# Twelve of 22 column groups of each up projection by seven products of block sums, in a float32 encoder block on one core

## The chip, the core and the metric

The kernel runs on one core of one Trainium2 chip. It is judged by device time in microseconds (us). A core has five engines that run beside each other, each with an instruction queue of its own that it works through in order: TensorE (PE in the profile; PEld is its weight load, which runs beside the matmul before it), VectorE (DVE), ScalarE (ACT), GpSimd (POOL) and SyncE (SP, which here only issues transfers). They wait for each other through semaphores. Operands lie in SBUF, matmul results in PSUM, which has eight banks of 128 x 512 float32 here.

## The reference, cut to what matters

One layer of a hybrid encoder on 256 tokens of 2048 features, float32. It begins and ends with a gated feed-forward network (FFN); the mixing layer and the cross-attention between them are not touched.

```
def swiglu(h, w_up, w_down):
    gate, up = jnp.split(h @ w_up, 2, axis=-1)
    return (jax.nn.silu(gate) * up) @ w_down
...
x = x + 0.5 * swiglu(rms_norm(x, ffn1_norm[l]), ffn1_w_up[l], ffn1_w_down[l])
...
x = x + 0.5 * swiglu(rms_norm(x, ffn2_norm[l]), ffn2_w_up[l], ffn2_w_down[l])
```

w_up is 2048 x 11264 (gate and up halves of 5632 columns), w_down is 5632 x 2048. Weights are read once per run, some 470 MB in all.

## The kernel before, in words

**Precision.** Every float32 matrix is split in two parts, h (rounded for the matmul) and l (the rest): `split` (L142) copies with ScalarE (L143) and subtracts with VectorE (L144). A float32 product is then three matmuls, h by h, h by l and l by h, which add up in PSUM; `three` (L396 to L404) issues them, with the activations as the stationary operand of 128 x 128 and the weights as the moving one.

**Pieces and steps.** In an FFN the 22 groups of an up projection are 256 gate and 256 up columns each. A group is four pieces: a piece is 1 MB of weights, 128 partitions x 2048 (four k tiles of 512 columns). The down projection has 11 blocks of four pieces, one for each quarter of the output. `ffn` (L411) goes through a list of steps, a piece each, which `ffn_order` (L45) makes: four steps of a group, and from time to time two blocks of the down projection, whose eight steps follow each other. Without fast groups an FFN has 88 up steps and 44 down steps, each of 24 matmuls of 512 columns (four k tiles, two halves of the tokens, three matmuls).

**Preparation.** `prepare` (L368) runs two pieces ahead: SP loads raw (three buffers), then the piece is split into an h and an l tile of 128 x 2048 (pools h and l, three buffers each, `FFN_POOLS`, L284). A buffer of raw is loaded again when its split has read it; one of h or l is written again when TensorE has read it. The transfer of a piece is issued by SP, in order.

**The end of a group.** After a group's fourth step `activate` (L421) computes silu(gate) x up from PSUM (ScalarE L429, VectorE L430); `turn` (L434), meant for two steps later, transposes the hidden block on TensorE (four transposes, L438) and splits it (L442, L443). A pair of down blocks is added into x from PSUM by VectorE (L514).

**The other branch.** The kernel has a second way to do a group, step kind "fast", which is not taken while FAST is 0. It treats two k tiles of activations and the group's 2 x 256 columns as 2 x 2 blocks. `operand_pairs` (L342) makes the activations' tiles; its inner `fast` adds four block sums of each pair (on VectorE, 128 x 128 each) and splits them. In `prepare` the weights' block sums go into a tile td, and h and l get seven blocks of 256 columns per pair of k tiles, so a fast piece fills two h and two l tiles. `ffn` issues the seven products by the table SEVEN (three matmuls of 256 columns each) into four banks, and after the fourth step adds the banks up on VectorE into a tile ev before `activate`.

**Order.** Each engine's order is not that of the source: a scheduler sets it when the kernel is built, and waits and buffers follow from it. The tiles of a piece alternate strictly among the three buffers.

**The FFNs' ends.** FFN1 begins with the load of x and its operands (`head_x`, `head_rest`, L525 to L541), quarter by quarter, mixed with the first four pieces; each quarter's source is a tile of the pool td. FFN2's operands are made while the attention's output projection runs.

Of the kernel before, what the change touches and what calls it, by code (L numbers as in the profile page):

```python
# [8 lines left out]
F32 = mybir.dt.float32  # L9
F32R = mybir.dt.float32r  # L10
ACT = mybir.ActivationFunctionType
ALU = mybir.AluOpType

P = 128
T = 256
# [3 lines left out]
FT = DFF // P  # L19
NU = DFF // 256  # L20
NB = FT // 4
FAST = 0
EPS = 1e-6
HEADS = 4
HD = D // HEADS
# [19 lines left out]
def ffn_order(fast):  # L45

    left = {"fast": fast, "up": NU - fast}  # L50
    begun = {"fast": None, "up": None}
    out, ended, down = [], [], []
    names = count()
    blocks = seen = 0

    def step(kind):
        if begun[kind] is None:
            begun[kind] = [next(names), 0]
            left[kind] -= 1
        g, i = begun[kind]  # L60
        out.append((kind, g, i))
        begun[kind] = [g, i + 1]
        if i == 3:
            ended.append(g)
            begun[kind] = None

    total = 4 * (NU + NB)
    while len(out) < total:
        fasts = sum(e[0] == "fast" for e in out)
        more = left["fast"] or begun["fast"]  # L70
        if more and fasts * (total - 12) < 4 * fast * (len(out) - 3):
            step("fast")
            continue
        if not down and not begun["up"]:
            ready = seen // 2 - blocks
            if ready >= 2 or (ready and not left["up"] and not more):
                n = min(2, ready)
                down = [("down", blocks, n, c, b) for c in range(4) for b in range(blocks, blocks + n)]
                blocks += n
        seen = len(ended)  # L80
        if down:
            out.append(down.pop(0))
        elif left["up"] or begun["up"]:
            step("up")
        elif more:
            step("fast")
    number = {g: i for i, g in enumerate(ended)}
    return [(e[0], number[e[1]], e[2]) if e[0] != "down" else e for e in out]
# [3 lines left out]
def block_kernel(ctx: ExitStack, tc: tile.TileContext, xT, xin, memT, vec, gfin, lruw, wu1, wd1, win, wv,  # L92
                 wab, wout, wq, wk, wvm, wo, wu2, wd2, out_):
    nc = tc.nc
    pe, dve, act, sp = nc.tensor, nc.vector, nc.scalar, nc.sync
# [9 lines left out]
    scoped = {}  # L105

    @contextmanager
    def scope(**pools):
        with ExitStack() as inner:
            for name, bufs in pools.items():  # L110
                scoped[name] = inner.enter_context(tc.tile_pool(name=name, bufs=bufs, reuse_waits="tile"))
            yield
            scoped.clear()

    def slot(dt=F32, name="slot"):
        return slots.tile([P, 1024], dt, name=name, tag="slot")
# [25 lines left out]
    def split(h, l, raw):  # L142
        act.activation(h, raw, ACT.Copy)  # L143
        dve.tensor_tensor(out=l, in0=raw, in1=h.bitcast(F32), op=ALU.subtract)  # L144
# [65 lines left out]
    def summed(acc, out=None, by=None):  # L210

        lo = t1("lo")
        act.activation(lo, acc[:, T:], ACT.Copy)
        out = t1("sum") if out is None else out
        dve.tensor_tensor(out=out, in0=acc[:, :T], in1=lo, op=ALU.add)
        if by is not None:
            dve.tensor_tensor(out=out, in0=out, in1=by, op=ALU.mult)
        return out
# [62 lines left out]
            dve.scalar_tensor_tensor(out=x[m], in0=half, scalar=by, in1=x[m], op0=ALU.mult, op1=ALU.add)  # L281


    FFN_POOLS = dict(h=3, l=3, td=2, ev=1, hd=2, tmp=4)  # L284

    class TokenSquares:

# [54 lines left out]
    def operand_pairs(src, gain, q, xg):  # L342

        out = []
        for i in range(2):
            for z in range(2):
                k = 2 * i + z
                act.activation(xg[i][:, z * T:][:, :T], src[:, k * T:(k + 1) * T], ACT.Copy,
                               scale=col(gain, 4 * q + k))
            h = slot(F32R, "xh")  # L350
            l = slot(F32R, "xl") if FAST else h[:, 512:]
            split(h[:, :512], l[:, :512], xg[i][:, :512])
            out.append((h, l))

        def fast():
            for s, (h, l) in zip(xg, out):
                for o, a, b, op in ((4, 1, 3, ALU.add), (5, 4, 0, ALU.subtract), (6, 1, 0, ALU.subtract),
                                    (7, 2, 5, ALU.subtract)):
                    o, a, b = (s[:, j * P:(j + 1) * P] for j in (o, a, b))
                    dve.tensor_tensor(out=o, in0=a, in1=b, op=op)  # L360
                split(h[:, 512:], l[:, 512:], s[:, 512:])

        return out, fast if FAST else lambda: None

    def split_pool(name):
        return scoped[name].tile([P, 2048], F32R, name=name, tag=name)

    def prepare(e, wu, wd, cuts=1):  # L368

        raw = rawp.tile([P, 2048], F32, name="raw", tag="raw")  # L370
        src = wd[e[4], e[3]] if e[0] == "down" else wu[e[1], e[2]]
        if e[0] != "fast":
            h, l = split_pool("h"), split_pool("l")
            n = 2048 // cuts
            for a in range(0, 2048, n):
                sp.dma_start(raw[:, a:a + n], src[:, a:a + n])
                split(h[:, a:a + n], l[:, a:a + n], raw[:, a:a + n])
            return h, l
        sp.dma_start(raw, src)
        out = []  # L380
        for i in range(2):
            b = raw[:, i * 1024:(i + 1) * 1024]
            td = scoped["td"].tile([P, 1024], F32, name="td", tag="td")
            b12, b22, b21 = b[:, :T], b[:, 512:768], b[:, 768:]
            dve.tensor_tensor(out=td[:, :512].rearrange("p (i n) -> p i n", i=2),
                              in0=b12[:, None, :].broadcast_to([P, 2, T]),
                              in1=b[:, 256:768].rearrange("p (i n) -> p i n", i=2), op=ALU.subtract)
            dve.tensor_tensor(out=td[:, 512:768], in0=b22, in1=td[:, :T], op=ALU.subtract)
            dve.tensor_tensor(out=td[:, 768:], in0=b21, in1=td[:, 512:768], op=ALU.subtract)
            h, l = split_pool("h"), split_pool("l")  # L390
            split(h[:, :768], l[:, :768], b[:, 256:])
            split(h[:, 768:1792], l[:, 768:1792], td)
            out.append((h, l))
        return out

# [15 lines left out]
    def ffn(order, wu, wd, pairs, sq, then, before=()):  # L411
# [42 lines left out]
        for e in order:  # L454
            while todo and len(ahead) < 2:
                i = len(order) - len(todo)
                if i < len(before):
                    before[i]()
                ahead.append(prepare(todo.pop(0), wu, wd, 4 if before and i == 0 else 1))
# [63 lines left out]
    fast1 = []  # L523

    def head_x(q):  # L525
        src = scoped["td"].tile([P, 1024], F32, name="xf", tag="td")
        n = 256 if q == 0 else 1024
        for a in range(0, 1024, n):
            sp.dma_start(src[:, a:a + n], xT[:, q * 1024 + a:][:, :n])
        new, fast = operand_pairs(src, "ffn1_norm", q, [slot(name="xg") for _ in range(2)])  # L530
        pairs1.extend(new)
        fast1.append(fast)

    def head_rest():
# [5 lines left out]
        for f in fast1:  # L540
            f()  # L541

    head = [lambda q=q: head_x(q) for q in range(4)] + [head_rest]


# [32 lines left out]
    xs2, sq2 = Operands(), TokenSquares()  # L578
    order1 = ffn_order(FAST)

# [7 lines left out]

    with scope(**FFN_POOLS):
        ffn(order1, wu1, wd1, pairs1, sq1, to_mix, head)  # L590
# [15 lines left out]
    def heads(t):  # L606
        return t.rearrange("p (h t) -> p h t", h=4)
# [3 lines left out]
    v = [scoped["extra"].tile([P, 1024], F32, name=f"v{t}", tag="extra") for t in range(2)]  # L611
# [230 lines left out]
    for m in range(KT):  # L842
# [3 lines left out]
        b = summed(parts[1], by=heads(gates[1, m // 4])[:, m % 4])  # L846
# [118 lines left out]

    with scope(**FFN_POOLS):
        ffn(ffn_order(FAST), wu2, wd2, pairs2, sq4, to_out)
        r = sq5.rstd_tokens()
# [96 lines left out]
```

## Time and profile before

| | |
|---|---|
| median of three runs | 2570.26 us (2565.64 to 2571.64) |
| the profiled execution: its own time, its span | 2569.93 us, 2568.2 us |
| TensorE busy, matmuls | 2531.1 us (99%), 12554 |
| VectorE, ScalarE busy | 1492.7 us (58%), 1209.3 us (47%) |
| chain that ended last | 95% TensorE |
| bytes read, mean rate | 470.10 MB, 184 GB/s |
| the two FFNs | about 7 to 757 us and 1821 to 2568 us of the span |

A row of the groups names line, engine, operation, out<-in, shapes and count; then total busy us, the mean ns of one, and the engine's idle time just before them with what ended it. A row of the timeline gives start and length in us, the engine, line, operation and tiles, xN for N merged ones, and in brackets the idle time before and who ended it. A matmul's length contains its way through the array, so consecutive ones overlap in the list; what one costs in a stream is the distance between starts. TensorE's granted clock is 0.995 of full speed on the mean.

### The profile page before, as it was taken

Reading aid. Unit: us, or ns where it says so; the run is one execution under the profiler, and the core shown is the slowest. Engines: PE = TensorE matmul, PEld = TensorE weight load, DVE = VectorE, ACT = ScalarE, POOL = GpSimd, SP = SyncE. Lnnn points to the kernel's source line nnn. Section 1 sums busy time; section 2 is a strip of 40 time slices with the busy share of each in tenths; the row PEclk is TensorE's granted clock in tenths of the full one; section 3 lists DMA queues with packets and bytes.
Section 4 is the critical chain, followed back from the end, with each engine's and each line's share of the span. In section 5 each row is a group of like instructions: output and inputs, shape, how many; then the busy total and the mean of one; then the engine's idle time right before and its main releaser. Section 6 shows DMA issues by size and latency. Waiting matters only on the chain.

```text
span 2568.2 us, 30319 instructions
## 1 busy us (share of the span) xinstructions
PE 2531.1 (99%) x12554; PEld 2132.7 (83%) x12554; DVE 1492.7 (58%) x1648; ACT 1209.3 (47%) x1416; POOL 0.2 (0%) x4
## 2 busy tenths in 40 slices
PE   7999999999999999999999999999999999999998
PEld 6888888888878888888888888888788888888886
DVE  5454545454555767776787776566445454545455
ACT  6434333434354444596555564555533334333333
POOL 0000000000000000000000000000000000000000
PEclk9999999999999999999999999999999999999999
DMA  7555555555535444454555555444555555555553
GB/s 267 193 187 194 192 186 195 188 189 196 183 146 196 164 164 151 166 178 178 186 191 190 204 200 194 164 148 164 190 187 195 184 194 191 186 196 187 191 195 133
DMA packets 68682, 474.16 MB, mean 185 GB/s; under 512 B 7616, under 2 KB 8384, under 8 KB 12352
## 3 DMA queue, kind: packets, MB, share of 16 engines
q1 hardware_dynamic: 68544, 472.23, 51.8%
q8 instruction: 98, 1.61, 0.2%
q14 instruction: 40, 0.33, 0.0%
HBM read 470.10 MB, written 2.10 MB: 184 GB/s over the span
## 4 chain that ended last, share of the span: by engine, by line
PE 95%; ACT 3%; DVE 1%; issue 0%; DMA 0%; SPq 0%; DVEq 0%; ACTq 0%
PE acc L198 20%; PE acc L404 19%; PE acc L402 18%; PE acc L403 18%; PE acc L199 10%; PE acc L656 2%; PE acc L658 2%; PE acc L657 2%; PE acc L438 1%; PE acc L720 1%; ACT wh L143 1%; ACT h L143 0%; DVE l L144 0%; ACT L796 0%; PE acc L932 0%
## 5 line engine op out<-in xcount | busy, mean ns | idle before, releaser
L144 DVE TENSOR_TENSOR l<-raw,h 128x2048 fp32r<-128x2048 f32 (+1 forms) x267 | 605.5, 2268 | 622.7 <-ACT h L143 621.6
L198 PE MATMUL acc<-ops,wh 128*128 128x512 f32 x2432 | 856.7, 397 | 1.0 <-ACT wh L143 0.9
L143 ACT ACTIVATE h<-raw 128x2048 fp32r<-128x2048 f32 (+1 forms) x267 | 506.4, 1897 | 733.7 <-PE acc L403 726.0
L199 PE MATMUL acc<-ops,wl 128*128 128x256 f32 x2432 | 680.7, 280 | 2.3 <-DVE wl L144 2.3
L144 DVE TENSOR_TENSOR wl<-raw,wh 128x1024 fp32r<-128x1024 f32 x352 | 430.2, 1224 | 264.8 <-ACT wh L143 262.7
L143 ACT ACTIVATE wh<-raw 128x1024 fp32r<-128x1024 f32 x352 | 372.4, 1059 | 414.8 <-PE acc L198 239.7
L402 PE MATMUL acc<-h,xh 128*128 128x512 f32 x1408 | 554.8, 394 | 11.5 <-ACT h L143 11.5
L404 PE MATMUL acc<-l,xh 128*128 128x512 f32 x1408 | 551.8, 392 | 5.3 <-DVE l L144 5.3
L403 PE MATMUL acc<-h,xh 128*128 128x512 f32 x1408 | 551.0, 391 | 0.0
L198 PEld LDWEIGHTS acc<-ops,wh 128*128 128x128 f32 x2432 | 456.7, 188 | 106.7 <-ACT wh L143 1.6
L199 PEld LDWEIGHTS acc<-ops,wl 128*128 128x128 f32 x2432 | 459.5, 189 | 4.1 <-DVE wl L144 3.6
L402 PEld LDWEIGHTS acc<-h,xh 128*128 128x128 f32 x1408 | 266.3, 189 | 67.3 <-ACT h L143 12.8
L404 PEld LDWEIGHTS acc<-l,xh 128*128 128x128 f32 x1408 | 266.2, 189 | 62.6 <-DVE l L144 6.7
L403 PEld LDWEIGHTS acc<-h,xh 128*128 128x128 f32 x1408 | 266.5, 189 | 54.5
L402 PE MATMUL acc<-h,hidop 128*128 128x512 f32 x704 | 275.2, 392 | 0.7 <-ACT hidop L442 0.7
L404 PE MATMUL acc<-l,hidop 128*128 128x512 f32 x704 | 274.3, 390 | 0.0
L403 PE MATMUL acc<-h,hidop 128*128 128x512 f32 x704 | 274.0, 389 | 0.0
L403 PEld LDWEIGHTS acc<-h,hidop 128*128 128x128 f32 x704 | 132.2, 188 | 27.8 <-DVE hidop L443 0.6
L402 PEld LDWEIGHTS acc<-h,hidop 128*128 128x128 f32 x704 | 132.1, 188 | 27.7 <-ACT hidop L442 1.1
L404 PEld LDWEIGHTS acc<-l,hidop 128*128 128x128 f32 x704 | 132.1, 188 | 27.6
L429 ACT ACTIVATE sg<-acc,rtok 128x256 f32<-128x256 f32 x88 | 40.9, 465 | 133.5 <-PE acc L404 133.5
L514 DVE SCALAR_TENSOR_TENSOR x<-acc,x 128x512 f32<-128x512 f32 x96 | 65.7, 691 | 37.6 <-PE acc L404 37.6
(189 smaller groups left out, 1352.4 us busy)
## 6 DMA issues: line engine op xcount, KB each, us to landing
raw<-wu SPq DMA_DIRECT2D x175, 1024.0 KB, 4.8
raw<-wd SPq DMA_DIRECT2D x88, 1024.0 KB, 4.8
raw<-win SPq DMA_DIRECT2D x72, 1024.0 KB, 4.8
raw<-wab SPq DMA_DIRECT2D x16, 1024.0 KB, 4.8
raw<-wout SPq DMA_DIRECT2D x16, 1024.0 KB, 4.8
raw<-wq SPq DMA_DIRECT2D x16, 1024.0 KB, 4.7
raw<-wk SPq DMA_DIRECT2D x16, 1024.0 KB, 4.8
raw<-wvm SPq DMA_DIRECT2D x16, 1024.0 KB, 4.7
```

The costliest lines, as they stand in the source:

```text
L143: act.activation(h, raw, ACT.Copy)
L144: dve.tensor_tensor(out=l, in0=raw, in1=h.bitcast(F32), op=ALU.subtract)
L198: pe.matmul(acc, h, x, start=start, stop=False)
L199: pe.matmul(acc[:, :T], l, x[:, :T], start=False, stop=stop)
L402: first = pe.matmul(acc, ah, bh, start=start, stop=False)
L403: pe.matmul(acc, al, bh, start=False, stop=False)
L404: return first, pe.matmul(acc, ah, bl, start=False, stop=stop)
L429: act.activation(sg, gate[t], ACT.Silu, scale=rstd[:, t:t + 1])
L514: dve.scalar_tensor_tensor(out=o, in0=accs["down"][t], scalar=0.5, in1=o, op0=ALU.mult, op1=ALU.add)
L656: pe.matmul(accs[t], xs[k][:, a:a + P], h, start=(k == 0), stop=False)
L657: pe.matmul(accs[t], xs[k][:, a:a + P], l, start=False, stop=False)
L658: pe.matmul(accs[t], xs[k][:, b:b + P], h, start=False, stop=(k == KT - 1))
```

## The change

FAST goes from 0 to 12: of each FFN's 22 groups, 12 are done by the fast branch. `ffn_order` spreads their 48 steps among the 40 remaining up steps and 44 down steps, after the first four steps of a group done the old way, so two steps in five are fast for most of an FFN (fast, other, fast, other, other). A fast step is 42 matmuls of 256 columns in place of 24 of 512. The weights' block sums of a whole piece are now made at once: td is one tile of 128 x 2048 in place of two of 1024, laid out like raw, so three VectorE instructions write all sums of a piece. The sources of x at the head of FFN1 come from the same pool, which now has one buffer. With FAST not 0, the l parts of the activations get tiles of their own, at the same columns as their h parts, and the block sums of the activations are made: in the head of FFN1, and for FFN2 in each quarter of the attention's output projection.

```
-FAST = 0
+FAST = 12
...
-    FFN_POOLS = dict(h=3, l=3, td=2, ev=1, hd=2, tmp=4)
+    FFN_POOLS = dict(h=3, l=3, td=1, ev=1, hd=2, tmp=4)
...
         sp.dma_start(raw, src)
+        td = scoped["td"].tile([P, 2048], F32, name="td", tag="td")
+        bv, tv = (v.rearrange("p (i j n) -> p i j n", i=2, j=4) for v in (raw, td))
+        dve.tensor_tensor(out=tv[:, :, :2], in0=bv[:, :, :1].broadcast_to([P, 2, 2, T]), in1=bv[:, :, 1:3],
+                          op=ALU.subtract)
+        dve.tensor_tensor(out=tv[:, :, 2], in0=bv[:, :, 2], in1=tv[:, :, 0], op=ALU.subtract)
+        dve.tensor_tensor(out=tv[:, :, 3], in0=bv[:, :, 3], in1=tv[:, :, 2], op=ALU.subtract)
         out = []
         for i in range(2):
-            b = raw[:, i * 1024:(i + 1) * 1024]
-            td = scoped["td"].tile([P, 1024], F32, name="td", tag="td")
-            b12, b22, b21 = b[:, :T], b[:, 512:768], b[:, 768:]
...
             h, l = split_pool("h"), split_pool("l")
-            split(h[:, :768], l[:, :768], b[:, 256:])
-            split(h[:, 768:1792], l[:, 768:1792], td)
+            split(h[:, :768], l[:, :768], raw[:, i * 1024 + 256:(i + 1) * 1024])
+            split(h[:, 768:1792], l[:, 768:1792], td[:, i * 1024:(i + 1) * 1024])
             out.append((h, l))
...
-        src = scoped["td"].tile([P, 1024], F32, name="xf", tag="td")
+        src = scoped["td"].tile([P, 2048], F32, name="xf", tag="td")[:, :1024]
```

The built kernel has 96 fast steps: per step three block-sum instructions on VectorE (1024, 512 and 512 columns) and four splits (768 and 1024 columns, twice).

More of the change, by code (lines that the diff above doesn't have):

```diff
@@ L379, in prepare @@
         sp.dma_start(raw, src)
+        td = scoped["td"].tile([P, 2048], F32, name="td", tag="td")
[4 more added lines that the diff above has]
+        dve.tensor_tensor(out=tv[:, :, 3], in0=bv[:, :, 3], in1=tv[:, :, 2], op=ALU.subtract)
         out = []
         for i in range(2):
-            b = raw[:, i * 1024:(i + 1) * 1024]
-            td = scoped["td"].tile([P, 1024], F32, name="td", tag="td")
-            b12, b22, b21 = b[:, :T], b[:, 512:768], b[:, 768:]
[L385 to L389, printed above, removed]
             h, l = split_pool("h"), split_pool("l")
-            split(h[:, :768], l[:, :768], b[:, 256:])
-            split(h[:, 768:1792], l[:, 768:1792], td)
+            split(h[:, :768], l[:, :768], raw[:, i * 1024 + 256:(i + 1) * 1024])
+            split(h[:, 768:1792], l[:, 768:1792], td[:, i * 1024:(i + 1) * 1024])
             out.append((h, l))
```

## The prediction

> **What bounds the kernel now.** I read the page first (busy shares, then the chain that ended last), then busy time by stage, then the groups kept apart by shape, and last the instructions in order of time where a price was wanted.
>
> ```profile
> span 2568.2 us, 30319 instructions
> ...
> PE 2531.1 (99%) x12554; PEld 2132.7 (83%) x12554; DVE 1492.7 (58%) x1648; ACT 1209.3 (47%) x1416; POOL 0.2 (0%) x4
> ...
> PE 95%; ACT 3%; DVE 1%; issue 0%; DMA 0%; SPq 0%; DVEq 0%; ACTq 0%
> ```
>
> TensorE carries 95% of the chain, so a change pays if it shortens TensorE's queue and leaves it fed. The two feed-forward stages (FFNs), the only place touched, are the first and last of these stretches (busy us of PE, PEld, DVE, ACT, POOL, then clock, DMA share, GB/s):
>
> ```profile
> 20.00:740.00 720.00, 715.15 (x3175) 589.54 (x3174) 361.06 (x244) 289.72 (x228) 0.00 (x0) 0.99 0.55 194
> ...
> 1840.00:2568.00 728.00, 716.69 (x3202) 592.37 (x3200) 366.17 (x257) 282.88 (x218) 0.00 (x0) 1.00 0.53 186
> ```
>
> There VectorE is half idle and ScalarE 60% idle. That idle time is what the change spends.
>
> **Prices.** Busy time of pipelined matmuls overlaps, so I take distances between starts.
>
> ```profile
> 199.76 0.39 PE L404 MATMUL acc<-l,xh 128*128 128x512 f32 x1
> ...
> 202.48 0.40 PE L404 MATMUL acc<-l,xh 128*128 128x512 f32 x1
> ```
> ```profile
> 1299.91 0.39 PE L198 MATMUL acc<-ops,wh 128*128 128x512 f32 x1
> ...
> 1303.37 0.39 PE L198 MATMUL acc<-ops,wh 128*128 128x512 f32 x1
> ```
> ```profile
> 864.87 0.39 PE L198 MATMUL acc<-ops,wh 128*128 128x512 f32 x1
> ...
> 865.93 0.40 PE L198 MATMUL acc<-ops,wh 128*128 128x512 f32 x1
> ```
> ```profile
> 862.62 1.87 PEld L720 LDWEIGHTS acc<-silu,k 128*128 128x128 f32 x16
> 864.41 0.19 PEld L198 LDWEIGHTS acc<-ops,wh 128*128 128x128 f32 x1
> ```
>
> The first pair is 12 matmuls of 512 columns apart: 2.72/12 = 0.2267 us each. The second is ten pairs of one 512 and one 256: 0.346 a pair, so a 256 costs 0.346 - 0.2267 = 0.119. The third, three such pairs, gives 0.353 and 0.127. The fourth: 16 weight loads under short matmuls in 1.79 us, 0.112 each, the floor for matmuls that each bring new weights. No row has 256 after 256; bounds 0.112 and 0.127, and I take 0.120, next to the ten-pair row, which has the same operand type.
>
> ```profile
> L144 DVE TENSOR_TENSOR l<-raw,h 128x2048 fp32r<-128x2048 f32 x263 | 602.8, 2292 | 621.4 <-ACT h L143 620.2 <-DMA x<-xin 1.1
> ...
> L143 ACT ACTIVATE h<-raw 128x2048 fp32r<-128x2048 f32 x263 | 503.9, 1916 | 732.1 <-PE acc L403 726.0 <-PE acc L198 4.1 <-DMA raw<-wu 2.1
> ...
> L144 DVE TENSOR_TENSOR wl<-raw,wh 128x1024 fp32r<-128x1024 f32 x352 | 430.2, 1224 | 264.8 <-ACT wh L143 262.7
> L143 ACT ACTIVATE wh<-raw 128x1024 fp32r<-128x1024 f32 x352 | 372.4, 1059 | 414.8 <-PE acc L198 239.7 <-issue 103.0 <-PE acc L658 50.2
> ...
> L514 DVE SCALAR_TENSOR_TENSOR x<-acc,x 128x512 f32<-128x512 f32 x96 | 65.7, 691 | 37.6 <-PE acc L404 37.6
> ...
> L430 DVE SCALAR_TENSOR_TENSOR hid<-acc,rtok,sg 128x256 f32<-128x256 f32 x88 | 42.3, 481 | 58.6 <-ACT sg L429 58.6
> ...
> L443 DVE TENSOR_TENSOR hidop<-acc,hidop 128x512 fp32r<-128x512 f32 x44 | 30.1, 684 | 2.7 <-ACT hidop L442 2.7
> ...
> L215 DVE TENSOR_TENSOR gate<-acc,lo 128x256 f32<-128x256 f32 x32 | 13.4, 418 | 1.7 <-ACT lo L213 1.7
> ...
> L144 DVE TENSOR_TENSOR xh<-xg,xh 128x512 fp32r<-128x512 f32 x16 | 11.1, 691 | 6.4 <-ACT xh L143 6.2
> ...
> L143 ACT ACTIVATE xh<-xg 128x512 fp32r<-128x512 f32 x16 | 10.1, 628 | 0.4
> ...
> L738 DVE TENSOR_TENSOR tots<-tots 128x128 f32<-128x128 f32 x2 | 0.6, 286 | 0.0
> ```
>
> VectorE: 0.69 for 512 columns, 1.22 for 1024, halfway, 0.96, for 768, 0.29 for 128. ScalarE: 1.06 for 1024, about 0.85 for 768 (between 0.63 and 1.06).
>
> **TensorE, per step.** A step of an up or down projection is 24 matmuls of 512: 5.44 us. A fast piece is 2 x 7 products of 3 matmuls, 42 of 256: 5.04 us. Gain 0.40; 96 fast pieces (12 groups x 4 x 2 FFNs): **-38.7** (-71 at 0.112, -10 at 0.127).
>
> The Trainium skill, page "TensorE: Matmul & The Clock Gate", section "Back-to-back issue gap", gives N/2.4 + 2.5 ns a warm matmul, 109 and 216 ns here. By it a fast piece would save 0.59 us and the sum would be -57; the 0.2267 us measured for 512 stands 11 ns above that rule.
>
> **Preparation.** An ordinary piece: one split, ScalarE 1.92 then VectorE 2.29. A fast one: block sums 1.22 + 2 x 0.69, then four splits, VectorE 2 x (0.96 + 1.22): 6.96 together, and ScalarE 2 x (0.85 + 1.06) = 3.8.
>
> ```profile
> 1822.99 0.69 DVE L144 TENSOR_TENSOR xh<-xg,xh 128x512 fp32r<-128x512 f32 x1 [2.34 <-ACT xh L143]
> 1823.60 2.29 DVE L144 TENSOR_TENSOR l<-raw,h 128x2048 fp32r<-128x2048 f32 x1
> ```
> ```profile
> 302.53 1.92 ACT L143 ACTIVATE h<-raw 128x2048 fp32r<-128x2048 f32 x1 [3.52 <-PE acc L403]
> ```
> ```profile
> 304.48 2.29 DVE L144 TENSOR_TENSOR l<-raw,h 128x2048 fp32r<-128x2048 f32 x1 [3.15 <-ACT h L143]
> ```
> ```profile
> raw<-wu SPq DMA_DIRECT2D x175, 1024.0 KB, 4.8
> ```
>
> Unwaiting VectorE work overlaps by 0.08 us, so a fast piece takes it 6.6. In the order of steps a group is ten steps: four fast, six ordinary. VectorE per group: 4 x 6.6 + 6 x 2.2 = 39.6; emptying four banks 3 x 0.69 + 0.42 = 2.5; 1.8 hidden blocks at 2 x 0.48 + 0.68 = 3.0; four residual adds 2.8: 48 us. TensorE: 4 x 5.04 + 6 x 5.44, and transposes (0.44 per hidden block, as before) 53.6. VectorE goes from half to nine tenths busy and still isn't the bound on average, so what counts is order.
>
> Walk through one group. With three h and l buffers and two per fast piece, the ordinary step behind a fast one can be split only from the fast step's start: 1.92 + 0.03 + 2.29 = 4.24 us, wanted at 5.04 + 0.45 (its third matmul is the first to read l). That fits by 1.2 us. But at two of four fast steps the built order puts the block sums of the next fast piece in front of that split on VectorE, and they wait for a transfer that starts only when the running piece's own raw was read. In the tightest case, counting from the start of the group's last fast step, the read ends at -2.45 (the buffer of its second half is free one ordinary step earlier, at -5.44; ScalarE's 0.85 lie beside VectorE's work on the first half, 0.96 and 1.22, which ends at -3.4; then 0.96), the transfer lands at 2.35 (4.8 us), sums to 3.6, split to 5.85, wanted at 5.49: 0.36 late. Then the banks: copy c, 0.69, an ordinary split 2.29 between, 0.42, 0.69, and sums of the next piece (2 x 0.69) woven in, 0.69, a split 0.96, hid 2 x 0.48: hid is done at 13.4, and the transposes, which stand after eight matmuls of the second ordinary step, reach TensorE at about 12.7: 0.6 lost with both waits; a second hidden block behind a 2.29 split loses 0.3. So 1.3 us where up pieces stand behind the group; with down pieces raw is read at -3.3 and nothing or 0.3 is lost. Over all I take 0.7 a group: **+17** for 24 groups (bounds 0 and 2.2 a group, +53, the rival below). Queued behind the late sums are that l split, the bank emptying and all later splits.
>
> **FFN1 start.**
>
> ```profile
> 26.57 2.29 DVE L144 TENSOR_TENSOR l<-raw,h 128x2048 fp32r<-128x2048 f32 x1 [1.11 <-DMA x<-xin]
> ```
> ```profile
> 17.14 0.50 PE L402 MATMUL acc<-h,xh 128*128 128x512 f32 x1 [2.26 <-ACT h L143]
> ```
> ```profile
> 37.44 0.39 PE L404 MATMUL acc<-l,xh 128*128 128x512 f32 x1
> 39.51 0.50 PE L402 MATMUL acc<-h,xh 128*128 128x512 f32 x1 [1.68 <-ACT h L143]
> ...
> 48.35 0.48 PE L402 MATMUL acc<-h,xh 128*128 128x512 f32 x1
> ```
> ```profile
> 17.00:25.00 8.00, 6.73 (x17) 5.10 (x18) 6.72 (x6) 7.87 (x15) 0.00 (x0) 0.58 0.97 346
> ...
> 41.50:46.00 4.50, 4.17 (x11) 3.34 (x12) 4.50 (x4) 1.92 (x2) 0.00 (x0) 0.62 0.69 248
> ```
>
> The fifth step starts at 39.51 now and the sixth at 48.35, the latter after a pause and a half clock that also go. In the changed order the fifth is the first fast piece. Behind the fourth split (done at 28.9, some 0.5 later now) VectorE has eight sums at 0.29, six operand splits at 0.69, the piece's block sums 2.6, two splits 0.96, an ordinary one 2.29, then the wanted 1.22: 14.4, and about 2 of waits for ScalarE: 45.7. TensorE, ready at 38.7 (37.7 now), idles 6.5 us and resumes at half clock (as the rows show after 2.3 us): fast piece done at 52.7, sixth step at 58.6, against 48.35 + 5.44 = 53.8 now. **+5** (3 to 10; the xT loads, now one buffer, also follow each other).
>
> **FFN2 start.** The last quarter's three more sums and one more operand split stand ahead of the first l split, which TensorE already waits for:
>
> ```profile
> 1825.94 1.22 PE L404 MATMUL acc<-l,xh 128*128 128x512 f32 x2 [3.14 <-DVE l L144]
> ```
>
> 3 x 0.29 + 0.69 = 1.6, and 1 for the other quarters: **+2.5** (0 to 4). The other quarters' work lies under 5.5 us per output tile of TensorE, of which VectorE uses some 3.3. Transfers, bytes and the down projections stay as they are, 0.
>
> **Sum.** -38.7 + 17 + 5 + 2.5 = -14.2, against the profiled execution's own 2569.93 us; the median 2570.26 is 0.3 above. 2556.
>
> **Rivals.** The first row is the transfers of the first 60 us.
>
> ```profile
> raw<-wu SPq DMA_DIRECT2D x11, 1024.0 KB, 7.9
> ```
>
> (1) Slower: the sums at the head of VectorE's queue. Place: the two fast steps per group, 48 in all, where they precede an ordinary split. For it: VectorE nine tenths busy, only 1.2 us of cover, and the same transfer at 7.9 us where many are in flight. Against: it lands in 4.8 in all steady parts, and DMA is half idle there. I have 8 us of the 17 for these places (0.17 each); 0.45 each brings no change, and 0.93 each (+44.6) gives 2592. (2) No change: a 256 at 0.1225 and 0.85 lost per group: -28.6 + 20 + 7.5, 2569. For it: the 0.127 row. (3) The 256 runs at the load floor 0.112: -71, with 1.05 lost per group (less cover) and 7.5: 2532. (4) Loads don't overlap: 42 x (0.112 + 0.120) = 9.7 us a fast step, +413, 2983. By that a 512 would take 0.34, and the rows show 0.227. The Trainium skill, same page, section "The mechanism", says that a weight load overlaps a running matmul only when its row group differs, which is this rival; the trace disagrees at full-height matmuls. That the change doesn't do what it says: the built order has 96 x 42 matmuls of 256 columns, so no.
>
> **Chances.** Forecast 0.43, (1) 0.33, (2) 0.15, (3) 0.08, (4) 0.01. Faster by over 0.2% (about what a measurement here can tell from no change, 5 us) is forecast and (3), 0.51; within 0.15; slower 0.34. Range 2530 to 2592: forecast, (2), most of (1) and of (3). The forecast's own range is 2545 to 2566 (0.1185 to 0.121 us, 0.5 to 0.95 per group).
>
> **What would show it.** Starts of L400 to L402 matmuls 0.12 apart and a fast step of 5.04; TensorE waits for l and hid under 1 us, few per group; a pause of some 6 us near 39 us. Wrong if waits for DVE l after fast steps sum to over 30 us, if VectorE waits for raw landings in the middle of the FFNs, if half-clock stretches appear there, or if the 256 lies outside 0.117 to 0.123.

## The result, and the profile after

The changed kernel takes 2540.39 us (median of four runs, 2538.34 to 2542.70), the kernel before 2570.70 us (median of four). The ratio is 0.9886, 95% interval 0.9869 to 0.9903: 30 us faster. The forecast was 2556, in the range 2530 to 2592. What TensorE gains came out as forecast; a loss that was forecast beside it did not come, so the sum was 16 us too high. The time also lies outside the forecast's own narrower range, 2545 to 2566. The profiled execution is the slowest of the four, 2542.7 us with a span of 2540.6; the profiled one of before had 2569.93 and 2568.2.

The page of the changed kernel's profiled execution (span, busy times, engines on the chain that ended last), and its busy time by stage with the columns as before:

```profile
span 2540.6 us, 35172 instructions
...
PE 2501.9 (98%) x14282; PEld 2188.1 (86%) x14282; DVE 1960.3 (77%) x2400; ACT 1390.9 (55%) x1744; POOL 0.2 (0%) x4
...
PE 95%; ACT 2%; DVE 1%; DMA 1%; issue 0%; DVEq 0%; ACTq 0%
```
```profile
60.00:740.00 680.00, 679.04 (x3959) 599.81 (x3958) 566.97 (x571) 361.19 (x369) 0.00 (x0) 1.00 0.54 194
```

TensorE still carries 95% of the chain. In the steady part of FFN1 it is busy 679 of 680 us at full clock, while VectorE has gone up to 83% (567 us). So the fast branch shortened TensorE's queue and did not starve it.

One fast step in the timeline (start, length, engine, line), from its first matmul to the first of the ordinary step behind it:

```profile
73.29 0.28 PE L400 MATMUL acc<-h,xh 128*128 128x256 f32 x1
73.41 0.28 PE L401 MATMUL acc<-h,xl 128*128 128x256 f32 x1
73.53 0.28 PE L402 MATMUL acc<-l,xh 128*128 128x256 f32 x1
...
78.21 0.28 PE L402 MATMUL acc<-l,xh 128*128 128x256 f32 x1
78.33 0.40 PE L400 MATMUL acc<-h,xh 128*128 128x512 f32 x1
```

42 matmuls take 78.33 - 73.29 = 5.04 us, 0.120 each. The median of the 96 fast steps is 5.033, of the ordinary steps before 5.440, so a fast step saves 0.407 us.

How long TensorE's sequence of steps took, from the starts of its matmuls (us):

| | before | after | difference |
|---|---|---|---|
| FFN1, start of its first step to the end of the sixth | 7.1 to 53.9 | 7.1 to 57.35 | +3.4 |
| FFN1, from there to the end | 702.5 | 682.2 | -20.3 |
| between the FFNs | 1065.2 | 1071.3 | +6.1 |
| FFN2, first step | 11.3 | 12.2 | +0.95 |
| FFN2, the rest | 724.05 | 705.2 | -18.9 |
| behind the last step | 11.25 | 12.35 | +1.1 |

The sum is, to rounding, the difference of the spans, 2540.6 - 2568.2 = -27.6. One of the rows is a surprise: in the stage between the FFNs TensorE has the same instructions in both kernels and took 6.1 us more. More on that at the end.

The steady parts hold 95 fast steps, 95 x 0.407 = 38.7, and became 39.2 us shorter. **On balance the groups lost nothing.** What TensorE's weight loads waited for in the steady part of FFN1 (who, for what: us in total, times, longest), and then VectorE:

```profile
PEld acc L325 <- DVE x L512: 1.5, 4, 0.5
PEld acc L325 <- issue: 1.2, 2, 0.6
PEld acc L402 <- DVE l L144: 1.1, 2, 0.8
PEld acc L436 <- DVE hid L428: 0.5, 2, 0.2
```
```profile
DVE l L144 <- ACT h L143: 51.9, 48, 3.2
DVE td L382 <- DMA raw<-wu: 26.3, 14, 3.8
```

VectorE does stand at the head of its queue waiting for transfers, as forecast (14 times in this stretch, 1.9 us each). But that wait reached TensorE almost nowhere: 1.1 us for l.

### The profile page after: what moved, and what is told of

Same layout as the page of the kernel before. It is cut to its first block, busy times and chain, and to the rows that moved or that the text cites. A ratio compares the mean times of both kernels' runs of the same rounds, so it can differ in the third digit from the quotient of the medians.

```text
span 2540.6 us, 35172 instructions
## 1 busy us (share of the span) xinstructions
PE 2501.9 (98%) x14282; PEld 2188.1 (86%) x14282; DVE 1960.3 (77%) x2400; ACT 1390.9 (55%) x1744; POOL 0.2 (0%) x4
## 4 chain that ended last, share of the span: by engine, by line
PE 95%; ACT 2%; DVE 1%; DMA 1%; issue 0%; DVEq 0%; ACTq 0%
PE acc L198 22%; PE acc L402 18%; PE acc L401 18%; PE acc L400 18%; PE acc L199 11%; PE acc L654 2%; PE acc L655 2%; PE acc L656 2%; PE acc L436 1%; PE acc L718 1%; DMA xf<-xT 1%; DVE l L144 0%; ACT wh L143 0%; PE acc L930 0%; PE acc L885 0%
## 5 line engine op out<-in xcount | busy, mean ns | idle before, releaser
L143 ACT ACTIVATE h<-raw 128x768 fp32r<-128x768 f32 (+2 forms) x363 | 484.4, 1335 | 458.5 <-PE acc L401 306.0
L400 PE MATMUL acc<-h,xh 128*128 128x256 f32 (+1 forms) x1984 | 635.8, 321 | 12.8 <-ACT h L143 12.8
L402 PE MATMUL acc<-l,xh 128*128 128x256 f32 (+1 forms) x1984 | 635.8, 321 | 7.4 <-DVE l L144 7.3
L144 DVE TENSOR_TENSOR l<-raw,h 128x768 fp32r<-128x768 f32 (+2 forms) x363 | 564.7, 1562 | 97.6 <-ACT h L143 97.1
L401 PE MATMUL acc<-h,xl 128*128 128x256 f32 (+1 forms) x1984 | 634.2, 320 | 0.0
L400 PEld LDWEIGHTS acc<-h,xh 128*128 128x128 f32 x1984 | 381.0, 192 | 40.9 <-ACT h L143 13.6
L402 PEld LDWEIGHTS acc<-l,xh 128*128 128x128 f32 x1984 | 380.9, 192 | 36.3 <-DVE l L144 10.1
L401 PEld LDWEIGHTS acc<-h,xl 128*128 128x128 f32 x1984 | 380.8, 192 | 27.5
L143 ACT ACTIVATE h<-td 128x1024 fp32r<-128x1024 f32 x192 | 198.9, 1050 | 158.4 <-DVE td L385 158.4
L144 DVE TENSOR_TENSOR l<-td,h 128x1024 fp32r<-128x1024 f32 x192 | 232.2, 1219 | 19.5 <-ACT h L143 18.6
L400 PEld LDWEIGHTS acc<-h,hidop 128*128 128x128 f32 x704 | 132.4, 188 | 25.7
```

What stands on the lines that cost most here:

```text
L400: first = pe.matmul(acc, ah, bh, start=start, stop=False)
L401: pe.matmul(acc, al, bh, start=False, stop=False)
L402: return first, pe.matmul(acc, ah, bl, start=False, stop=stop)
```

## The experiments

The question was why the groups lost nothing where 0.7 us each was forecast. Theory A: the waits are there and the cover is a little larger than worked out, so it is thin, and order decides. Theory B: VectorE has idle time, and order matters little. The runs then went on to the start of FFN1 and to more fast groups. All times by stage below are from the starts of TensorE's matmuls in each run's own trace; the changed kernel has 732.5 us for FFN1 and 717.4 for FFN2.

### One block sum made twice

```diff
         dve.tensor_tensor(out=tv[:, :, :2], in0=bv[:, :, :1].broadcast_to([P, 2, 2, T]), in1=bv[:, :, 1:3],
                           op=ALU.subtract)
+        dve.tensor_tensor(out=tv[:, :, :2], in0=bv[:, :, :1].broadcast_to([P, 2, 2, T]), in1=bv[:, :, 1:3],
+                          op=ALU.subtract)
```

> The first and largest of a fast piece's three block sums (1.22 us on VectorE) is made twice; nothing else changes. Theory A (thin cover): in the changed kernel the groups lose nothing because the l split behind a fast step is done 0.4 to 0.9 us before TensorE reads it at two of four fast steps, and hid 0.5 us before the transposes. 1.14 us more at the head of VectorE's queue overruns both, so about 0.24 + 0.6 at the splits and some 0.5 at the transposes, 1 to 1.3 us a group: 24 to 32 us over the changed kernel's 2540, 2560 to 2575, and the trace shows TensorE waiting for VectorE's l behind fast steps. Theory B (VectorE is a fifth idle in the feed-forward stages, so its order does not matter): 96 x 1.14 = 109 us of work go into the 270 us in which it is idle, under 3 us longer, 2540 to 2543.

2558.41 us, ratio to the kernel before 0.9954 (0.9939 to 0.9969): 18 us more than the changed kernel. FFN1 743.0, FFN2 727.1, 20 us more in the two. The timeline of this run, VectorE and TensorE at a second fast step of a group (in brackets the idle time before and who ended it; lines stand two lower in this kernel):

```profile
219.79 0.69 DVE L387 TENSOR_TENSOR td<-raw,td 128x512 f32<-128x512 f32 x1
221.61 2.36 DVE L144 TENSOR_TENSOR l<-td,h 128x1024 fp32r<-128x1024 f32 x2 [1.13 <-ACT h L143]
```
```profile
221.85 0.28 PE L403 MATMUL acc<-h,xl 128*128 128x256 f32 x1
222.89 0.39 PE L404 MATMUL acc<-l,xh 128*128 128x256 f32 x1 [0.76 <-DVE l L144]
```

(The doubled instruction writes the same values again.) TensorE waits for the split of the fast piece's own block sums (those of its first half), 0.9 us a time, at the second fast step of 11 of the 24 groups; one group in each stage loses 2.6, there at an ordinary piece, and the start of FFN1 ends 2.0 us later. So theory A holds in kind: 109 us of work put into VectorE's idle time cost 20 us, not 3. Its place was not the one I named. The scheduler built another order, which kept nearly all splits of the ordinary pieces in time, and the split of td, which mostly had 2.4 us to spare at that step in the changed kernel, was the one overrun.

### The block sums as they were

```diff
-    FFN_POOLS = dict(h=3, l=3, td=1, ev=1, hd=2, tmp=4)
+    FFN_POOLS = dict(h=3, l=3, td=2, ev=1, hd=2, tmp=4)
...
+            td = scoped["td"].tile([P, 1024], F32, name="td", tag="td")
+            b12, b22, b21 = b[:, :T], b[:, 512:768], b[:, 768:]
+            dve.tensor_tensor(out=td[:, :512].rearrange("p (i n) -> p i n", i=2),
+                              in0=b12[:, None, :].broadcast_to([P, 2, T]),
+                              in1=b[:, 256:768].rearrange("p (i n) -> p i n", i=2), op=ALU.subtract)
+            dve.tensor_tensor(out=td[:, 512:768], in0=b22, in1=td[:, :T], op=ALU.subtract)
+            dve.tensor_tensor(out=td[:, 768:], in0=b21, in1=td[:, 512:768], op=ALU.subtract)
```

> Twelve fast groups as in the changed kernel, but the block sums as before the change: per half of a piece, six instructions on two buffers of half the size, in place of three on one. VectorE has 2 x 0.69 + 4 x 0.42 = 3.06 us in place of 2.60 a piece, 44 us in all. Theory A (thin cover, 0.4 to 0.9 us at the tightest splits): 0.46 us more takes up nearly all of it, 0 to 0.4 us lost a group, 2540 to 2550; first-half sums stand alone at the head of the queue, which gives some back. Theory B (idle time covers it): 2540, within 2 us. The middle stage and the start of the second feed-forward stage stay as they are in the changed kernel by both.

So this run is the kernel before with FAST = 12 and nothing else changed. 2539.14 us, ratio 0.9882 (0.9867 to 0.9897), not to be told from the changed kernel. By stage it is 733.1 and 718.6, 1.7 us longer, as both theories allow; the middle stage was 4.4 us shorter here, by which the whole came out no slower. What the change gains is the twelve fast groups; the three large sums in place of six small ones bring 1.7 us by these two traces, which the whole times do not show.

### A later start, and then later transposes

```diff
-def ffn_order(fast):
+def ffn_order(fast, skip=3):
...
-        if more and fasts * (total - 12) < 4 * fast * (len(out) - 3):
+        if more and fasts * (total - 12) < 4 * fast * (len(out) - skip):
...
-    order1 = ffn_order(FAST)
+    order1 = ffn_order(FAST, 6)
```

> The order of steps of the first feed-forward stage alone: its first fast piece becomes the eighth step (near 59 us) in place of the fifth (38 us). All 96 fast steps stay. Theory A (the start costs 3.4 us net, because the first fast piece waits for VectorE's activation sums and block sums and then runs at half clock): the sixth step ends near 53.9 us as in the kernel before, and the whole is 3 to 4 us shorter, 2536 to 2537. Rival: the pause is the activation sums themselves, and the ordinary fifth and sixth steps find VectorE as late: no change within 1 us.

2547.52 us, ratio 0.9921 (0.9901 to 0.9941): slower than the changed kernel. Both theories missed. The start did gain, and more than hoped: the sixth step is done at 49.78 us, in place of 57.35, and of 53.91 before any change. But FFN1 as a whole took 742.2 us, 9.7 more. The waits of TensorE's weight loads in the steady part of FFN1, and a place in the timeline:

```profile
PEld acc L436 <- DVE hid L428: 13.0, 7, 5.0
PEld acc L436 <- issue: 5.5, 4, 1.8
```
```profile
322.33 0.39 PE L402 MATMUL acc<-l,hidop 128*128 128x512 f32 x1
323.98 0.33 PE L436 MATMUL acc<-vt,hid 128*128 128x128 f32 x1 [1.26 <-DVE hid L428]
```

Nine times (the expectation below has ten) TensorE stands before the transposes (L436) of a hidden block: from the matmul before to the transpose it is 1.3 to 1.8 us and once 4.9, where 0.23 is usual, 15.7 us in all. In the new order the scheduler had put these nine 24 matmuls behind the group's last fast step; in the changed kernel most stand 32 behind. Eight matmuls are 1.8 us, and that is about the wait. The next run moves only that.

```diff
-            late.append((2, lambda: turn(g, hid)))
+            late.append((3, lambda: turn(g, hid)))
```

> The later start of the run before (first fast piece as the eighth step of the first feed-forward stage), and in both stages the transposes of a hidden block are put into TensorE's queue one step later (after three steps in place of two). In the run with the later start alone TensorE stood before the transposes ten times in the first stage, 1.3 to 1.8 us each and once 4.9, because they stood 24 matmuls behind the last fast step in place of 32 and VectorE's hid came after them. Theory A (the loss is the place of the transposes): these 18 us go, the start's gain of 7.6 us (sixth step done at 49.8 in place of 57.35) stays, first stage 724 to 728 us in place of 742 and of 732.5 in the changed kernel, second stage 717 as it is; whole 2531 to 2537. Theory B (VectorE is simply late behind a fast group when a residual add falls there): the wait moves to the l splits behind, first stage over 735, whole over 2541.

2526.44 us, ratio 0.9833 (0.9816 to 0.9849): 14 us faster than the changed kernel, 44 faster than the one before. FFN1 723.8, FFN2 716.7. By the two traces 8.7 us of the gain over the changed kernel lie in FFN1, and 6.5 in the stage between the FFNs, which this edit does not touch. All that TensorE's weight loads still wait for in the same stretch of FFN1, hid no longer among it:

```profile
PEld acc L325 <- DVE x L512: 1.9, 5, 0.5
PEld acc L199 <- DVE wl L144: 1.4, 2, 1.1
PEld acc L325 <- issue: 1.2, 2, 0.6
PEld acc L198 <- ACT wh L143: 0.9, 1, 0.9
```

In FFN2, whose order of steps is that of the changed kernel, the edit changed hardly anything (717.4 in the changed kernel, 716.8 in the run with the later start). That it was not VectorE's order that got better can be read from the same traces. In the changed kernel, with the later start and here, hid is done 12.3 us after the start of its group's last fast step (median of the 24 groups); TensorE comes to the transposes at 12.3 us in the changed kernel (median), at 10.5 in all nine late cases of the run before, and at 15.95 here (median). Theory A: the loss was the place of the transposes, not VectorE's work.

### Fourteen fast groups

```diff
-FAST = 12
+FAST = 14
```

> 14 fast groups of 22 in place of 12, 16 fast steps more; the order becomes fast and ordinary steps in turn. TensorE gains 16 x 0.407 = 6.5 us. Theory A (thin cover): for a group of eight steps with two hidden blocks VectorE has 26.4 + 8.8 + 2.5 + 3 + 2.8 = 43.5 us against TensorE's 42.8, so it is the bound there, 0.7 to 1.5 us lost in each of 28 groups: 2553 to 2575, and TensorE waits for l. Theory B (average idle covers it, VectorE 639 us of 705 a stage): 2533 to 2535.

2572.67 us, ratio 1.0008 (0.9999 to 1.0017): the whole gain is gone. FFN1 748.7, FFN2 734.0, against 732.5 and 717.4, with 6.5 us less of matmuls. Theory A by its number, and again the wait is not the one named: TensorE (weight loads, then matmuls) stands for hid, hardly for l. (The two lists tell of the same waits, so 9.6 and 11.5 do not make the 21 us of which the next expectation speaks. From start to start the waits before late transposes are 12.8 us in FFN1 and 12.1 in FFN2.)

```profile
PEld acc L436 <- DVE hid L428: 9.6, 11, 1.8
PEld acc L436 <- issue: 6.3, 4, 1.8
PEld acc L400 <- ACT h L143: 4.5, 2, 2.2
...
PEld acc L402 <- DVE l L144: 1.0, 2, 0.6
```
```profile
PE acc L436 <- DVE hid L428: 11.5, 11, 1.4
```

So the same edit, transposes one step later, with 14 groups:

> 14 fast groups in each stage as in the run of that number, and the transposes one step later in TensorE's queue. With 14 alone the first stage took 748.7 us and the second 734.0, and TensorE waited 21 us for hid in the first. Theory A (place of the transposes): these waits go, 728 and 714 us, whole 2531 to 2537. Theory B (VectorE is the bound where fast and ordinary steps stand in turn, 43.5 us of work to TensorE's 42.8): the waits go over to l, half or more of the loss stays, whole 2545 to 2560.

2528.22 us, ratio 0.9844 (0.9827 to 0.9861); FFN1 726.8, FFN2 714.4. Theory A: one edit took some 42 us out of the two stages. 25 of them are the waits seen at the transposes; two waits for h of 2.0 us in each stage went too, and how these and the rest hang on the transposes was not followed. VectorE's busy time in the steady part of FFN1 (third of the busy columns), at 14 groups, first with the early and then with the late transposes:

```profile
60.00:740.00 680.00, 664.37 (x4027) 592.10 (x4026) 596.30 (x607) 364.52 (x369) 0.00 (x0) 1.00 0.55 192
```
```profile
60.00:740.00 680.00, 678.57 (x4120) 607.21 (x4118) 606.50 (x633) 378.55 (x405) 0.00 (x0) 1.00 0.56 194
```

VectorE is busier (89%) in the run that loses next to nothing than in the one that loses 20 us a stage (88%): it has the same work in a longer stage. The share said nothing about the loss; the order did.

### A sum on GpSimd

```diff
-        dve.tensor_tensor(out=tv[:, :, 3], in0=bv[:, :, 3], in1=tv[:, :, 2], op=ALU.subtract)
+        nc.gpsimd.tensor_tensor(out=tv[:, :, 3], in0=bv[:, :, 3], in1=tv[:, :, 2], op=ALU.subtract)
```

> As the kernel before it, and the third block sum of a fast piece (0.69 us on VectorE) is made by GpSimd, which is idle; no row shows what it takes there. Theory A (VectorE not the bound once the transposes stand later): no change to the kernel before it, within 3 us. Theory B (VectorE is the bound): 2.8 us of 43.5 go in each group, VectorE falls below TensorE's 42.8, and at up to about 2 us a sum on GpSimd most of the waits for l go, 2533 to 2540; at over 4 us a sum the last split of each half comes late and it is slower than the kernel before it.

2573.29 us, ratio 1.0015 (1.0003 to 1.0026): 45 us worse than the same kernel with the sum on VectorE. Neither theory. FFN1 748.7, FFN2 736.5. The groups by shape in the steady part of FFN1, VectorE's splits without and with the sum on GpSimd, and GpSimd's sum (busy us, mean ns):

```profile
L144 DVE TENSOR_TENSOR l<-raw,h 128x768 fp32r<-128x768 f32 x108 | 102.6, 953 | 0.7 <-ACT h L143 0.7
```
```profile
L144 DVE TENSOR_TENSOR l<-raw,h 128x768 fp32r<-128x768 f32 x108 | 121.2, 1125 | 0.0
```
```profile
L385 POOL TENSOR_TENSOR td<-raw,td 128x512 f32<-128x512 f32 x53 | 115.2, 2173 | 509.1 <-DVE td L384 431.5 <-ACT h L143 59.1 <-ACT sg L427 18.5
```

And this run's busy times in the same stretch (the fifth is GpSimd's):

```profile
60.00:740.00 680.00, 664.53 (x4029) 593.01 (x4028) 596.43 (x555) 363.45 (x369) 115.17 (x53) 1.00 0.56 192
```

36.5 us of sums (53 x 0.69) left VectorE in this stretch, and its busy time fell by 10.1 only, from 606.5 to 596.4, although the slower run has less of its stage in the stretch. Over the whole run, where the other work is the same, 77.1 us of sums left, and the lengths of all of VectorE's instructions together fell by 10.2: others of them got longer. Of 63 splits of 768 columns that met a sum on GpSimd, 29 took 2.05 us; one alone takes 0.95. And the sum itself takes 2.2 us there on the mean (0.69 on VectorE; a span on GpSimd is rough): 1.3 in 48 of the 112, over 3 in 41. It ends up on the way to the last split. The Trainium skill, page "SBUF — State Buffer", section "SBUF: two separate sides", says that a VectorE instruction with two SBUF inputs and a GpSimd one that reads SBUF shut each other out for the whole instruction; the doubled splits agree. How much of the 45 us is that and how much the order that the scheduler built for it was not separated.

### Both edits with 14, and 16 groups

```diff
-FAST = 12
+FAST = 14
...
-def ffn_order(fast):
+def ffn_order(fast, skip=3, rest=12):
...
-        if more and fasts * (total - 12) < 4 * fast * (len(out) - 3):
+        if more and fasts * (total - rest) < 4 * fast * (len(out) - skip):
...
-            late.append((2, lambda: turn(g, hid)))
+            late.append((3, lambda: turn(g, hid)))
...
-    order1 = ffn_order(FAST)
+    order1 = ffn_order(FAST, 6, 14)
```

> 14 fast groups in each stage, the first fast piece of the first stage as the eighth step, and the transposes one step later. Theory A (the terms add): the first stage as with the later start at 12 groups, 723.8, less 8 x 0.407 and plus about 1 us lost (as the second stage showed at 14: 714.4 against 716.7, 2.3 gained of 3.3), 721.5; second stage 714.4; 4.7 us less than 2526.4: 2520 to 2523, up to 5 more if the middle stage falls into its slower rhythm. Theory B (VectorE with hardly any idle time left makes the gains not add): 2526 or more in the same rhythm.

2527.61 us, ratio 0.9829 (0.9816 to 0.9842), not to be told from 12 groups with the same edits. Against that kernel FFN2 gained 3.2 us (713.5), more than forecast; FFN1 gained nothing (723.75) where 2.3 was, and the stage between them was 3.1 us longer. The gains add in one stage and not in the other. In FFN1 the trace shows a start that took 0.6 us more and three waits of 0.5 to 0.6 us, for l and hid, that the other kernel does not have; why they arise stays open.

With 16 and the transposes later, at the old start:

```diff
-FAST = 12
+FAST = 16
...
-            late.append((2, lambda: turn(g, hid)))
+            late.append((3, lambda: turn(g, hid)))
```

> 16 fast groups in each stage with the transposes one step later, the first fast piece as the fifth step as in the changed kernel. Now nine fast pieces of a stage follow a fast one directly. TensorE gains 32 x 0.407 = 13 us over 12 groups. Theory A (VectorE counts by queue, place by place): two fast pieces in a row ask 13.2 us of VectorE in 10.07 us of TensorE, about 2 us lost at each such pair, 36 us in all, slower than with 14: 2540 to 2560. Theory B (only the sum over a stage counts, 679 us of VectorE in 703): 2520 to 2527.

2552.29 us, ratio 0.9926 (0.9912 to 0.9939), theory A; FFN1 737.5, FFN2 724.8. In FFN1 two fast pieces follow each other at eight places (the expectation has nine). The largest waits, for h and then l, stand behind four of them, 2.3 us each:

```profile
214.60 0.50 PE L400 MATMUL acc<-h,hidop 128*128 128x512 f32 x1 [1.14 <-ACT h L143]
...
216.93 0.73 PE L402 MATMUL acc<-l,hidop 128*128 128x512 f32 x2 [0.88 <-DVE l L144]
```

The lowest median of all is that with 12 groups, a later start in FFN1 and the later transposes, 2526.44 us; 14 groups with one or both of these edits (2528.22 and 2527.61) cannot be told from it.

## Why the prediction was right where it was, and wrong where it was

**What bounds: right.** TensorE was the bound and stayed so. VectorE is busy 83% where the sum for a group gave nine tenths.

**Fast steps: right.** 0.120 us for a 256 was taken and 0.1198 measured; the term of -38.7 (-38.5 by its own prices) is 96 x 0.407 = -39.1. Rival (2) with 0.1225, rival (3), the load floor of 0.112, and rival (4), loads that don't overlap, are out.

**Groups: the step that failed.** +17 (0.7 a group) was taken, -0.5 for all 24 measured. (The -0.5 is what is left over of the steady parts. It holds 2.7 us of slower matmuls behind fast steps, told at the end, and some 3 us less of waits at the FFNs' ends.) This is a mis-sized term, and the walk can be checked against the trace at the very group it was made for, the first, whose last fast step starts at 83.79 us. VectorE:

```profile
79.47 0.95 DVE L144 TENSOR_TENSOR l<-raw,h 128x768 fp32r<-128x768 f32 x1
...
85.44 1.23 DVE L382 TENSOR_TENSOR td<-raw 128x1024 f32<-128x1024 f32 x1 [1.14 <-DMA raw<-wu]
...
86.98 2.28 DVE L144 TENSOR_TENSOR l<-raw,h 128x2048 fp32r<-128x2048 f32 x1
...
96.04 0.48 DVE L428 SCALAR_TENSOR_TENSOR hid<-ev,rtok,sg 128x256 f32<-128x256 f32 x1 [0.26 <-ACT sg L427]
```

And TensorE:

```profile
88.93 0.49 PE L436 MATMUL acc<-vt,hid 128*128 128x128 f32 x3
89.18 0.48 PE L400 MATMUL acc<-h,xh 128*128 128x512 f32 x1
89.50 0.39 PE L401 MATMUL acc<-h,xl 128*128 128x512 f32 x1
89.73 0.40 PE L402 MATMUL acc<-l,xh 128*128 128x512 f32 x1
```

| from the start of the group's last fast step | walk | trace |
|---|---|---|
| raw read to the end | -2.45 | -3.37 (80.42) |
| sums begin (transfer landed) | 2.35 | 1.65 |
| split of the ordinary piece done | 5.85 | 5.48 (89.27) |
| l wanted by TensorE | 5.49 | 5.94 (89.73) |
| hid done | 13.4 | 12.7 (96.52) |

The order and the wait for the transfer were right at this place. The read of raw ended 0.9 us earlier than walked, because VectorE was done earlier with the splits of that piece's first half; of this 0.37 us was left at the ordinary split, as the transfer took 5.0 us in place of 4.8 and half of another hidden block stood before the split. And TensorE came 0.45 later, mostly because the transposes of that hidden block (L436, 0.36 us) stand at the end of this fast step, which the walk had left out. So 0.36 late became 0.46 early, and hid, 0.7 late in the walk (13.4 against 12.7), was in time. The same holds elsewhere: at 22 of the 24 groups the split behind the last fast step is done 0.3 to 0.6 us before it is read. The lower bound of the term, 0, was the right value; the forecast put a loss of tenths into a place where an error of 0.8 us in the walk decides.

Rival (1), the sums at the head of VectorE's queue, got 0.33. Its wait stands at 29 places, not 48: behind the last fast step of 22 groups and the second of 7, since at the others the built order has the split first, or no fast piece follows. Its price was next to nothing: TensorE's weight loads wait 1.6 us for l in the steady parts of both FFNs. The runs with the doubled sum, with 14 and with 16 groups show that a loss of that size was near, a little more work or another order costing 18 to 44 us, but with waits at other places than the rival's: for the split of td, for hid, and behind two fast pieces in a row.

**FFN1 start: right in kind.** The sixth step was forecast to end at 58.6 and ended at 57.35, +3.4 against before where +5 was taken. The pause, and the clock (the column behind the five engines' busy times):

```profile
38.40:43.00 4.60, 1.31 (x6) 0.67 (x4) 4.60 (x6) 4.39 (x5) 0.00 (x0) 1.00 0.25 50
43.00:52.00 9.00, 7.42 (x42) 7.42 (x43) 6.83 (x9) 3.60 (x6) 0.00 (x0) 0.62 0.54 218
```

VectorE is busy throughout the first stretch (third busy time) and TensorE for 1.3 of 4.6 us; then comes a clock of 0.62, as described.

**FFN2 start.** +2.5 was taken, +0.95 measured.

**The sum.** Against -14.2: nothing from the fast steps (95 of them are 38.7; the first lies in the row of the start), 17.5 us less from the groups, 1.6 and 1.55 less from the starts, and 7.2 us the other way between the FFNs and behind the last step, which the sum had at 0: -27.6. That these 7.2 us brought the result nearer to the forecast is luck: 6.1 of them lie in a stage whose time, as far as the traces show, the change did not set. Without them it would be some 2533 us, at the end of the range that was there for rival (3), whose mechanism is out.

**One of the signs was badly chosen.** "VectorE waits for raw landings in the middle of the FFNs" was to show the forecast wrong; it came true (26.3 us in FFN1 alone) and cost next to nothing. What was telling was TensorE's own wait.

## What to carry to other kernels

When an idle engine is filled up, its share of busy time does not say whether the bound engine will wait: 88% lost 20 us a stage and 89% next to nothing, with the same work in another order. Where a walk through the order gives a few tenths late or early, give the term both values and say which is likelier, because an instruction left out of it (here four transposes) is as large as the result. And before paying for a waiting producer, look whether the consumer can stand later in its queue: here one step later for the transposes decided over more time than two more fast groups could save.

## What the runs showed of the hardware that was not expected

**A stream of 512 and 256 columns in turn has several rhythms.** In the stage between the FFNs TensorE has the same instructions in all runs, and took 1064.8 to 1071.3 us. In the kernel before, the rows at 1299.91 and 1303.37 us quoted in the prediction are ten pairs, 0.346 each. The changed kernel, ten pairs near that place:

```profile
1285.12 0.40 PE L198 MATMUL acc<-ops,wh 128*128 128x512 f32 x1
...
1288.65 0.40 PE L198 MATMUL acc<-ops,wh 128*128 128x512 f32 x1
```

0.353 each, at full clock and with no wait shown. In the one the starts repeat every pair (346 or 347 ns), in the other every three pairs (349, 350 and 361 ns), for 200 us and more. A kernel changes between them on its way: the prediction's row at 864.87 us, which it took as an upper bound for the price of a 256, shows the slower one in the kernel before. Over the whole stage the 2385 such pairs take 842.0 us in the kernel before and 848.2 in the changed one, 6.2 us more, which is the whole difference. Before, after and the nine further runs had 1065.2, 1071.3, 1066.8, 1066.9, 1066.0, 1066.9, 1064.8, 1070.5, 1065.4, 1067.9 and 1066.8 us there, whatever was done in the FFNs; the run with the block sums as they were has the same twelve fast groups as the changed kernel and 4.4 us less. So the 6.1 us of the profiled difference can't be put down to the change, with one trace of each kernel. What starts one rhythm or the other stays open; no run was made for it.

**Behind a run of short matmuls the first long ones are slower.** Of the ordinary steps behind a fast one, the first five matmuls take about 0.03 us more in all (5.468 us a step in the median, 5.440 before), with no wait shown: 2.7 us over the 96 such steps.
